# The first norm of the last token block: x turned on TensorE instead of loaded feature by feature

## The chip, the core and the metric

The kernel runs on one core of a Trainium2 chip. The metric is the device time of one execution in microseconds (us). Before the change it is 2847.49 us, the median of three runs (2845.23 to 2849.25).

## What is computed

One layer of an encoder: 2048 tokens, 1024 features, all float32. The part around the change is the first norm and what takes it up:

```python
def rms_norm(x, g):
    xf = x.astype(jnp.float32)
    y = xf * lax.rsqrt(jnp.mean(xf * xf, axis=-1, keepdims=True) + EPS)
    return (y * g.astype(jnp.float32)).astype(x.dtype)

def modulate(h, shift, scale):
    return h * (1 + scale) + shift
...
        h = modulate(rms_norm(x, norm_g[i, 0]), sh_m, sc_m)
        if m == 0:
            y = stick_breaking_mixer(h, sb_w_qkv[r], sb_w_o[r])
...
    qkv = (h @ w_qkv).reshape(b, s, 3, N_HEADS, HEAD_DIM)
```

`stick_breaking_mixer` is an attention of 16 heads whose weights come from sigmoids of the scores and a running product along the keys, in blocks of 128 queries. It is followed by an output projection, a gate and a gated feed-forward layer.

## The kernel before, in words

Every product is done in two or three passes on float32 data split into a high part (rounded) and a low part (the rest): a high and a low half are kept side by side in one tile, and `mm3` (lines 176 to 178) runs high x high, high x low, low x high. So each operand costs a rounding copy (high) and a subtraction (low) on some engine.

The tokens are cut into four blocks of 512 (b = 0 to 3), the features into eight groups of 128 (k = 0 to 7), the heads into eight pairs. `project` makes keys (t = 1), queries (t = 0) and values (t = 2) of one pair and one block: eight slices of three matmuls each, `pj`. The projections of pair 0 for blocks 0 to 3 come first. Beside them the norm of the next block is made, and with block 1 the attention of pair 0 begins: from then on slices of projections and stages of attention alternate in a fixed order that is written out by hand (`ORDER_IN_SLOT`). All four compute engines issue in exactly the order in which the program records their instructions; only the DMA queue SP is ordered by the framework.

The stages of attention, for each 128 queries and 512 keys: `score` (TensorE, `z`, line 604), `sigmoids` (ScalarE, two passes: `a` line 621, `z` in place line 623), `break_sticks` (VectorE scan into `w`, lines 633 and 638; then GpSimd multiplies `a` by it, line 645), `turn` (TensorE transposes, `t`, line 655), `split_high` (ScalarE copy, `aT`, line 665), `split_low` (VectorE subtraction, `aT`, line 671), `weigh_values` (TensorE, `o`, line 683). The values are turned as well (`vt`, line 552) and split (`v`, lines 556 and 557).

PSUM has eight banks of 128x512: three for the scores (`z`), two for the turned weights (`t`) and three (`acc`) shared by the projection (`pj`), the attention output (`o`), the turned values (`vt`) and, where there are any, the turned x (`xT`).

The norm has two ways. Blocks 0 and 2 go by tokens: x is loaded with tokens on the partitions, squared and summed on ScalarE (line 167), scaled by its reciprocal root on VectorE (line 349, 128x1024 each) and turned on TensorE, one feature group at a time (`x_turn`, line 372). For block 2, ScalarE then applies scale and shift (`hf`, line 394), and VectorE makes the high part (line 395) and the low part (line 396). Blocks 1 and 3, those in `BY_FEATURES`, go by features: x is also loaded with features on the partitions (`cols_load`, line 324, four DMAs `xc`), the reciprocal roots are spread over 128 columns (line 351), turned once (`xr`, line 363) and copied to SBUF (line 365). Each feature group is then multiplied by that row, on VectorE for even k (line 383) and on GpSimd for odd k (line 387). The modulated high part is ScalarE's (line 400, or lines 405 and 406), the low part VectorE's (line 401) or, for odd k of block 3, GpSimd's (line 408).

`first_norm` does this for one group. For block 3 it is called for k = 0 to 2 during the values' slices of block 2 (`NORM_AT[3]`), and for k = 3 to 7 during the keys' slices of block 3, three slices ahead of the slice that needs the group.

Of the kernel before, what the change touches and what calls it, by code (L numbers as in the profile page):

```python
# [9 lines left out]
F32 = mybir.dt.float32  # L10
F32R = mybir.dt.float32r
AF = mybir.ActivationFunctionType
ALU = mybir.AluOpType
# [3 lines left out]
P = 128  # L17
D = 1024
S = 2048
KC = D // P  # L20
# [3 lines left out]
BT = 512  # L24
NB = S // BT
# [44 lines left out]

H2_STEP = 3

BY_FEATURES = (1, 3)

SQUARE_AT = [(0, 2), (0, 7), (2, 1), (2, 7)]

# [7 lines left out]
def f32(ap):  # L84
    return ap.bitcast(F32)
# [22 lines left out]
def hybrid_trunk_kernel(  # L108
# [16 lines left out]
    nc = tc.nc  # L125
# [57 lines left out]
    tps = ctx.enter_context(tc.tile_pool(name="tps", bufs=2, space=PSUM))  # L183
    accps = ctx.enter_context(tc.tile_pool(name="accps", bufs=3, space=PSUM))
# [136 lines left out]
    def cols_load(b):  # L321
        for m in range(KC // 2):
            cols = att.tile([P, 2, BT], F32, name=f"xc{b}_{m}", tag="kt", bufs=BUFS["kt"])
            nc.sync.dma_start(cols, xt[b // 2, :, 2 * m : 2 * m + 2])
            x_cols[b, 2 * m], x_cols[b, 2 * m + 1] = cols[:, 0], cols[:, 1]

    def x_square(b, i):
        if b > 0:
            tok = x_tiles[b, i]
            if b in BY_FEATURES:  # L330
                junk = tok
# [13 lines left out]
    def x_spread(b, i):  # L345

        if b not in BY_FEATURES:
            tok = x_norm[b, i] = x_tiles.pop((b, i))
# [6 lines left out]
    def x_share(b):  # L355

        if b not in BY_FEATURES:
            return
        pool, tag = (tps, "t") if b < 2 else (accps, "acc")
        pt = pool.tile([P, BT], F32, name=f"xr{b}", tag=tag)  # L360
        for i in range(4):
            tok = x_tiles.pop((b, i))
            nc.tensor.transpose(pt[:, i * P : (i + 1) * P], tok[:, :P], ident)
        x_row[b] = tok[:, BT:]
        nc.scalar.copy(x_row[b], pt)

    def x_turn(b, k):

        pool, tag = (tps, "t") if b == 0 else (accps, "acc")
        pt = pool.tile([P, BT], F32, name=f"xT{b}_{k}", tag=tag)  # L370
        for i in range(4):
            nc.tensor.transpose(
                pt[:, i * P : (i + 1) * P], x_norm[b, i][:, k * P : (k + 1) * P], ident
            )
        return pt

    def scale_cols(b, k):

        if b not in BY_FEATURES:
            return  # L380
# [8 lines left out]
    def modulate(hl, b, k):  # L389

        gain, add = g_eff[:, 0, k : k + 1], shift[:, 0, k : k + 1]
        if b not in BY_FEATURES:
            u = att.tile([P, BT], F32, name=f"hf{b}_{k}", tag="tmp", bufs=BUFS["tmp"])
            nc.scalar.activation(u, x_turn(b, k), AF.Identity, bias=add, scale=gain)
            nc.vector.tensor_copy(hl[:, 0], u)
            nc.vector.tensor_tensor(hl[:, 1], u, f32(hl[:, 0]), op=ALU.subtract)
            return
        u = x_cols.pop((b, k))
        if k % 2 == 0:
            nc.scalar.activation(hl[:, 0], u, AF.Identity, bias=add)  # L400
            nc.vector.scalar_tensor_tensor(
                hl[:, 1], u, add, f32(hl[:, 0]), op0=ALU.add, op1=ALU.subtract
            )
        else:
            nc.scalar.activation(u, u, AF.Identity, bias=add, scale=gain)
            nc.scalar.copy(hl[:, 0], u)
            eng = nc.gpsimd if b == NB - 1 else nc.vector
            eng.tensor_tensor(hl[:, 1], u, f32(hl[:, 0]), op=ALU.subtract)  # L408

    def h_load(p, b):  # L410
        h = []
# [8 lines left out]
    def first_norm(b, k):  # L420
        if b is None or k >= KC:
            return
        if k % 2 == 0:
            ht = att.tile([P, 2, 2, BT], F32R, name=f"ht0_{b}_{k // 2}", tag="ht", bufs=BUFS["ht"])
            norm_h.setdefault(b, []).extend([ht[:, 0], ht[:, 1]])
            norm_tile[b] = ht
        for ahead in range(0 if k == 0 else k + 2, min(k + 3, KC)):
            scale_cols(b, ahead)
        modulate(norm_h[b][k], b, k)
        if k % 2 == 1:  # L430
            nc.sync.dma_start(h_s[b][:, k - 1 : k + 1], f32(norm_tile[b]))
# [21 lines left out]
    def project(at):  # L453

        p, b = STEPS[at]
# [3 lines left out]
        nb = STEPS[at + 1][1] if at + 1 < len(STEPS) and STEPS[at + 1][0] == 0 else None  # L459
# [4 lines left out]
        def product(t):  # L464
            if begun:
                return first_acc[t]
            w = weights[p, t]
            if parked and t == 1:
                acc = zps.tile([P, BT], F32, name=f"pj{p}_{b}_{t}", tag="z")
            else:  # L470
                acc = accps.tile([P, BT], F32, name=f"pj{p}_{b}_{t}", tag="acc")
            ahead = b == NB - 1 and p + 1 < NPAIR
            for k in range(KC):
                if t == 1:
                    if p == 0:
                        first_norm(b, k + (4 if b == 1 else 3))
                    if k == 0 and nb == 3:
                        cols_load(3)
                    if k == 5 and waiting:
                        waiting.pop()()  # L480
                if parked and t == 1 and k % 2 == 0:
                    nc.sync.dma_start(*stores[k // 2])
                if parked and (t, k) == (1, 6):
                    split_early(1, 2, ["whl"])
                if nb in (1, 3) and t == 1 and k < 4:
                    x_square(nb, k)
                if nb and t == 1 and 2 <= k < 6:
                    x_spread(nb, k - 2)
                if nb == 2 and (t, k) == (0, 0):
                    x_load(3)  # L490
                if nb == 1 and (t, k) in SQUARE_AT:
                    x_square(2, SQUARE_AT.index((t, k)))
                if nb and (t, k) == (0, 1):
                    x_share(nb)
                if (t, k) in NORM_AT[nb]:
                    first_norm(nb, NORM_AT[nb].index((t, k)))
                if ahead and k == 0:
                    load_weights(p + 1, t)
                if ahead and k == 6:
# [34 lines left out]
        else:  # L534
# [311 lines left out]
    for q in range(4):  # L846
        m = 2 * q
# [632 lines left out]
    for n, (s, f) in enumerate(groups):  # L1480
# [3 lines left out]
        for at, product in enumerate(PRODUCTS):  # L1484
            acc = banks_of[{1: 0, 6: 0, 7: 0, 4: 0, 5: 1, 3: 1, 2: 2}[product]]
            for k in range(H4):
                hl, r = left[n - (n == FC), product], right[s, product, k]
# [3 lines left out]
                t = 4 * at + k  # L1491
# [220 lines left out]
```

## Time and profile before

| | us |
|---|---|
| median of three runs | 2847.49 |
| the profiled execution | 2847.32 |
| its span, first to last instruction | 2845.3 |
| TensorE busy in the span | 2797.2 |
| VectorE busy | 2025.0 |
| ScalarE busy | 1634.2 |
| GpSimd busy | 1288.2 |

PE is TensorE's matmuls, DVE is VectorE, ACT is ScalarE, POOL is GpSimd, SP is the queue that issues the DMAs. The granted TensorE clock is 0.999 of full speed on the mean. A timeline row gives start, duration (both us), engine, line of the kernel, operation, tiles written and read, their size and count; in brackets how long the engine was idle before it and what ended that. A wait row gives the waiting group, the one it waited for, the us in total, how many times, and the longest.

### The profile page before, as it was taken

How to read it: one execution, taken by the hardware profiler on the slowest of the kernel's cores; microseconds unless marked ns; L12 is line 12 of the kernel's file. 1: busy time of each engine (PE TensorE's matmuls, PEld its weight loads, DVE VectorE, ACT ScalarE, POOL GpSimd, SP SyncE). 2: the span in 40 equal slices, each digit the busy share in tenths (PEclk: the TensorE clock that was granted, in tenths of full speed). 3: DMA queues.
4: the chain of work that ended last, by engine and by line, in shares of the span. 5: the costliest groups of instructions: out<-in, count | busy, mean ns of one | idle time of the engine just before them, and what ended most of it. 6: DMA issues, size and time to landing. Idle time of an engine off the chain costs nothing.

```text
span 2845.3 us, 41773 instructions
## 1 busy us (share of the span) xinstructions
PE 2797.2 (98%) x13825; PEld 2335.3 (82%) x13825; DVE 2025.0 (71%) x2824; ACT 1634.2 (57%) x3275; POOL 1288.2 (45%) x2036
## 2 busy tenths in 40 slices
PE   8999999999999999999999999999999999999998
PEld 6788888888888888887888788888788888888887
DVE  6788898888888888888866766655776655133376
ACT  5787777788777877777645533333433333322233
POOL 1475666666575655657410122221222222544454
PEclk9999999999999999999999999999999999999999
DMA  9865547657565635646289644334453335545566
GB/s 359 291 219 167 189 151 231 210 170 235 182 211 193 202 123 179 201 127 236 80 304 313 207 137 152 123 94 161 134 175 110 111 105 166 191 139 154 181 212 200
DMA packets 240520, 521.04 MB, mean 183 GB/s; under 512 B 22448, under 2 KB 110512, under 8 KB 222640
## 3 DMA queue, kind: packets, MB, share of 16 engines
q1 hardware_dynamic: 240304, 518.38, 56.1%
q8 instruction: 109, 1.79, 0.3%
q14 instruction: 107, 0.88, 0.1%
HBM read 351.04 MB, written 118.49 MB: 165 GB/s over the span
## 4 chain that ended last, share of the span: by engine, by line
PE 85%; DVE 5%; issue 3%; ACT 2%; POOL 2%; DMA 2%; SPq 0%; DVEq 0%; POOLq 0%; ACTq 0%
PE s L176 9%; PE s L177 9%; PE s L178 9%; PE z L604 8%; PE o L683 8%; PE t L655 8%; PE pj L176 5%; PE pj L177 5%; PE pj L178 5%; PE o L178 4%; PE o L177 4%; PE o L176 4%; PE y L178 2%; PE y L176 2%; PE y L177 2%
## 5 line engine op out<-in xcount | busy, mean ns | idle before, releaser
L645 POOL TENSOR_TENSOR a<-a,w 128x512 f32<-128x512 f32 (+3 forms) x640 | 621.1, 970 | 225.3 <-DVE w L638 130.4
L638 DVE TENSOR_TENSOR_SCAN w<-z,c,begin 128x512 f32<-128x512 f32 x384 | 489.4, 1279 | 84.7 <-ACT z L623 62.1
L176 PE MATMUL s<-r,l 128*128 128x512 f32 x1232 | 481.8, 391 | 4.8 <-DVE p L1447 3.9
L178 PE MATMUL s<-r,l 128*128 128x512 f32 x1232 | 479.9, 389 | 0.0
L177 PE MATMUL s<-r,l 128*128 128x512 f32 x1232 | 479.8, 389 | 0.0
L621 ACT ACTIVATE a<-z 128x512 f32<-128x512 f32 (+3 forms) x640 | 347.1, 542 | 170.7 <-PE z L604 137.6
L683 PE MATMUL o<-aT,v 128*128 128x512 f32 (+3 forms) x1280 | 384.8, 382 | 0.1
L671 DVE TENSOR_TENSOR aT<-t,aT 128x512 fp32r<-128x512 f32 (+3 forms) x640 | 358.8, 595 | 23.7 <-ACT aT L665 23.1
L604 PE MATMUL z<-kt,qt 128*128 128x512 f32 (+3 forms) x1280 | 363.8, 366 | 0.1
L665 ACT CAST aT<-t 128x512 fp32r<-128x512 f32 (+3 forms) x640 | 314.0, 533 | 73.8 <-PE t L655 63.7
L623 ACT ACTIVATE z<-z 128x512 f32<-128x512 f32 (+3 forms) x640 | 345.5, 540 | 0.0
L1455 POOL TENSOR_TENSOR one<-p,p 128x512 f32<-128x512 f32 x44 | 71.5, 1624 | 576.7 <-issue 320.3
L176 PE MATMUL pj<-ht,w 128*128 128x512 f32 x768 | 309.5, 403 | 5.0 <-issue 1.4
L655 PE MATMUL t<-begin,a 128*128 128x128 f32 x2176 | 295.9, 274 | 14.1 <-DVE aT L671 12.9
L655 PEld LDWEIGHTS t<-begin,a 128*128 128x128 f32 x2176 | 255.5, 140 | 64.8 <-DVE aT L671 15.6
L177 PE MATMUL pj<-ht,w 128*128 128x512 f32 x768 | 303.7, 395 | 1.8 <-DVE ht L408 0.6
L178 PE MATMUL pj<-ht,w 128*128 128x512 f32 x768 | 303.3, 395 | 0.0
L176 PEld LDWEIGHTS s<-r,l 128*128 128x128 f32 x1232 | 231.3, 188 | 54.8 <-ACT l L1308 2.9
L178 PEld LDWEIGHTS s<-r,l 128*128 128x128 f32 x1232 | 231.3, 188 | 48.1
L177 PEld LDWEIGHTS s<-r,l 128*128 128x128 f32 x1232 | 231.4, 188 | 47.9 <-issue 0.5
L633 DVE TENSOR_TENSOR_SCAN w<-z,begin 128x128 f32<-128x128 f32 (+3 forms) x256 | 208.8, 818 | 77.0 <-ACT z L623 66.3
L604 PEld LDWEIGHTS z<-kt,qt 128*128 128x128 f32 x1280 | 230.6, 189 | 37.8 <-DVE w L633 0.5
(179 smaller groups left out, 4881.6 us busy)
## 6 DMA issues: line engine op xcount, KB each, us to landing
ht<-h_s SPq DMA_DIRECT2D x108, 1024.0 KB, 8.5
wi<-in_win SPq DMA_DIRECT2D x86, 512.0 KB, 4.0
qt<-qn SPq DMA_DIRECT2D x124, 256.0 KB, 4.9
ol_qt<-act_s SPq DMA_DIRECT2D x56, 512.0 KB, 3.9
act_s<-S SPq DMA_DIRECT2D x66, 256.0 KB, 3.9
br<-in_wout SPq DMA_DIRECT2D x66, 256.0 KB, 3.5
h_s<-ht SPq DMA_DIRECT2D x16, 1024.0 KB, 8.3
o_s<-os SPq DMA_DIRECT2D x128, 128.0 KB, 3.0
```

Source lines behind the costliest of these rows:

```text
L176: nc.tensor.matmul(acc, lhs[0], rhs[0], start=first, stop=False, **kw)
L177: nc.tensor.matmul(acc, lhs[0], rhs[1], start=False, stop=False, **kw)
L178: nc.tensor.matmul(acc, lhs[1], rhs[0], start=False, stop=last, **kw)
L604: nc.tensor.matmul(z[:, :n], q[:, e, part, r * P : (r + 1) * P], k[:, e, :n], start=part == 0, stop=part == 1,)
L621: nc.scalar.activation(a[:, :n], z[:, :n], AF.Sigmoid, scale=QK_SCALE)
L623: nc.scalar.activation(z[:, :n], z[:, :n], AF.Sigmoid, scale=-QK_SCALE)
L638: nc.vector.tensor_tensor_scan(rest[:, rev], left[:, rev], begin[:, :BT][:, rev], initial=carries[r], op0=ALU.mult, op1=ALU.bypass,)
L645: nc.gpsimd.tensor_tensor(a[:, :n], a[:, :n], rest[:, 1 : n + 1], op=ALU.mult)
L655: nc.tensor.transpose(pt[:, rb * P : (rb + 1) * P], weighed[i, rb][:, j * P : (j + 1) * P], ident)
L665: nc.scalar.copy(hl[:, 0, t0:], pt[:, t0:])
L671: nc.vector.tensor_tensor(hl[:, 1, t0:], pt[:, t0:], f32(hl[:, 0, t0:]), op=ALU.subtract)
L683: nc.tensor.matmul(acc[:, t0:], lhs, hl[:, part, t0:], start=sc == qb and j == 0 and part == 0, stop=sc == 0 and j == 3 and part == 1,)
```

## The change

Block 3 leaves `BY_FEATURES` and goes by tokens, like block 2, but with another split of the work: VectorE applies scale and shift straight from PSUM, ScalarE makes the high part, GpSimd the low part. The column loads of block 3, its spread roots and the row of roots are gone. The squares of block 3 are written to a tile of the `wraw` buffers instead of over x, since x is still needed.

```diff
-BY_FEATURES = (1, 3)
+BY_FEATURES = (1,)
...
-        pool, tag = (tps, "t") if b < 2 else (accps, "acc")
-        pt = pool.tile([P, BT], F32, name=f"xr{b}", tag=tag)
+        pt = tps.tile([P, BT], F32, name=f"xr{b}", tag="t")
...
         if b not in BY_FEATURES:
             u = att.tile([P, BT], F32, name=f"hf{b}_{k}", tag="tmp", bufs=BUFS["tmp"])
+            if b == NB - 1:
+                nc.vector.tensor_scalar(u, x_turn(b, k), gain, add, op0=ALU.mult, op1=ALU.add)
+                nc.scalar.copy(hl[:, 0], u)
+                nc.gpsimd.tensor_tensor(hl[:, 1], u, f32(hl[:, 0]), op=ALU.subtract)
+                return
             nc.scalar.activation(u, x_turn(b, k), AF.Identity, bias=add, scale=gain)
...
             nc.scalar.copy(hl[:, 0], u)
-            eng = nc.gpsimd if b == NB - 1 else nc.vector
-            eng.tensor_tensor(hl[:, 1], u, f32(hl[:, 0]), op=ALU.subtract)
+            nc.vector.tensor_tensor(hl[:, 1], u, f32(hl[:, 0]), op=ALU.subtract)
...
-                    if k == 0 and nb == 3:
-                        cols_load(3)
```

On TensorE 32 transposes of 128x128 come (eight groups of four) and four go; on VectorE eight passes come for eight; on ScalarE eight copies for twelve passes and the copy of the row; on GpSimd eight subtractions for four multiplications and four subtractions; on SP four loads of 512 KB go.

The order at three places, by the built programs. First VectorE during the keys' product of block 2, where the tokens of block 3 are scaled (`x3_2` and `x3_3` are the third and fourth 128 of them, `ht0_2` is block 2's normed x, `w1` and `t0` belong to attention units 1 and 0). Before:

```order
L396 TENSOR_TENSOR ht0_2_3_1016<-hf2_7_1036,ht0_2_3_1016 128x512
L351 TENSOR_SCALAR x3_2_795<-ones_68,n0_3_2_rstd_1000 128x128
L633 TENSOR_SCALAR w1_1_1050<-z1_1_1013,begin_62 128x256
L351 TENSOR_SCALAR x3_3_797<-ones_68,n0_3_3_rstd_1030 128x128
L633 TENSOR_SCALAR w1_2_1076<-z1_2_1057,begin_62 128x384
L671 TENSOR_TENSOR aT0_0_1083<-t0_0_1067,aT0_0_1083 128x512
L508 TENSOR_TENSOR kn0_2_1092<-pj0_2_1_929,kn0_2_1092 128x512
L671 TENSOR_TENSOR aT0_1_1104<-t0_1_1072,aT0_1_1104 128x384
```

and after (line numbers are one higher from there on):

```order
L400 TENSOR_TENSOR ht0_2_3_1011<-hf2_7_1032,ht0_2_3_1011 128x512
L349 TENSOR_SCALAR x3_2_795<-x3_2_795,n0_3_2_rstd_995 128x1024
L634 TENSOR_SCALAR w1_1_1046<-z1_1_1008,begin_62 128x256
L349 TENSOR_SCALAR x3_3_797<-x3_3_797,n0_3_3_rstd_1026 128x1024
L634 TENSOR_SCALAR w1_2_1072<-z1_2_1053,begin_62 128x384
L672 TENSOR_TENSOR aT0_0_1079<-t0_0_1063,aT0_0_1079 128x512
L509 TENSOR_TENSOR kn0_2_1088<-pj0_2_1_929,kn0_2_1088 128x512
L672 TENSOR_TENSOR aT0_1_1100<-t0_1_1068,aT0_1_1100 128x384
```

Nothing moves; the four scalings (two are shown) grow from 128x128 to 128x1024 in place.

Second, VectorE during the keys' product of block 3, where groups 5, 6 and 7 are made (`w5`, `t3`, `t4` are attention stages). Before:

```order
L638 TENSOR_SCALAR w5_0_1480<-z5_0_1460,c4_0_1369,begin_62 128x512
L671 TENSOR_TENSOR aT3_2_1487<-t3_2_1470,aT3_2_1487 128x512
L401 TENSOR_SCALAR ht0_3_3_1503<-xc3_3_946,shift_74,ht0_3_3_1503 128x512
L671 TENSOR_TENSOR aT3_3_1509<-t3_3_1475,aT3_3_1509 128x512
L638 TENSOR_SCALAR w5_1_1512<-z5_1_1492,c4_1_1392,begin_62 128x512
L638 TENSOR_SCALAR w5_2_1540<-z5_2_1521,c4_2_1416,begin_62 128x512
L671 TENSOR_TENSOR aT4_0_1547<-t4_0_1531,aT4_0_1547 128x512
```

and after:

```order
L639 TENSOR_SCALAR w5_0_1496<-z5_0_1470,c4_0_1374,begin_62 128x512
L672 TENSOR_TENSOR aT3_2_1503<-t3_2_1486,aT3_2_1503 128x512
L394 TENSOR_SCALAR hf3_5_1511<-xT3_5_1512,g_eff_73,shift_74 128x512
L394 TENSOR_SCALAR hf3_6_1525<-xT3_6_1526,g_eff_73,shift_74 128x512
L672 TENSOR_TENSOR aT3_3_1537<-t3_3_1491,aT3_3_1537 128x512
L639 TENSOR_SCALAR w5_1_1540<-z5_1_1508,c4_1_1397,begin_62 128x512
L394 TENSOR_SCALAR hf3_7_1552<-xT3_7_1553,g_eff_73,shift_74 128x512
L639 TENSOR_SCALAR w5_2_1574<-z5_2_1549,c4_2_1421,begin_62 128x512
L672 TENSOR_TENSOR aT4_0_1581<-t4_0_1565,aT4_0_1581 128x512
```

A pass over a turned group now stands ahead of each scan or subtraction there, where one low part stood. On ScalarE the copies `ht0_3` of these passes stand in the same way between the sigmoids and the high parts; before, its scalings of `xc` stood there.

Third, TensorE in the same slices. Before, two slices of the keys' product follow each other:

```order
L604 MATMUL z5_1_1492<-kt0_0_531,qt0_1_826 128x512 x2
L176 MATMUL pj0_3_1_1435<-ht0_3_1_1329,w0_1_279 128x512
L177 MATMUL pj0_3_1_1435<-ht0_3_1_1329,w0_1_279 128x512
L178 MATMUL pj0_3_1_1435<-ht0_3_1_1329,w0_1_279 128x512
L176 MATMUL pj0_3_1_1435<-ht0_3_1_1329,w0_1_279 128x512 [waits Activation_49]
L177 MATMUL pj0_3_1_1435<-ht0_3_1_1329,w0_1_279 128x512 [waits Pool_49]
```

and after (`xT3_5` and `xT3_6` are groups 5 and 6 of block 3, both in the same PSUM bank):

```order
L605 MATMUL z5_1_1508<-kt0_0_531,qt0_1_826 128x512 x2
L371 MATMUL xT3_5_1512<-begin_62,x3_0_791 128x128 [waits DVE_49]
L371 MATMUL xT3_5_1512<-begin_62,x3_1_793 128x128
L371 MATMUL xT3_5_1512<-begin_62,x3_2_795 128x128
L371 MATMUL xT3_5_1512<-begin_62,x3_3_797 128x128
L176 MATMUL pj0_3_1_1440<-ht0_3_1_1328,w0_1_279 128x512
L177 MATMUL pj0_3_1_1440<-ht0_3_1_1328,w0_1_279 128x512
L178 MATMUL pj0_3_1_1440<-ht0_3_1_1328,w0_1_279 128x512
L371 MATMUL xT3_6_1526<-begin_62,x3_0_791 128x128 [waits DVE_49]
L371 MATMUL xT3_6_1526<-begin_62,x3_1_793 128x128
L371 MATMUL xT3_6_1526<-begin_62,x3_2_795 128x128
L371 MATMUL xT3_6_1526<-begin_62,x3_3_797 128x128
```

Ahead of each slice stands a group of four transposes, and each group waits for VectorE: `xT3_3` to `xT3_7` are all given one bank of the `acc` pool, because the projection and the attention output hold the other two.

More of the change, by code (lines that the diff above doesn't have):

```diff
@@ L323, in cols_load @@
             cols = att.tile([P, 2, BT], F32, name=f"xc{b}_{m}", tag="kt", bufs=BUFS["kt"])
-            nc.sync.dma_start(cols, xt[b // 2, :, 2 * m : 2 * m + 2])
+            nc.sync.dma_start(cols, xt[:, 2 * m : 2 * m + 2])
             x_cols[b, 2 * m], x_cols[b, 2 * m + 1] = cols[:, 0], cols[:, 1]
@@ L1686 @@
         "x": get("x")[0],
-        "xt": get("x")[0].reshape(NB, BT, KC, P).transpose(0, 3, 2, 1)[1::2],
+        "xt": get("x")[0].reshape(NB, BT, KC, P).transpose(0, 3, 2, 1)[1],
         "c": get("c")[0].reshape(KC, P).T,
```

## The prediction

> **What bounds the kernel now.** I read the page first (busy time, then the chain that ended last), then the stretch that the change touches: by windows, by waits, by timeline.
>
> ```profile
> span 2845.3 us, 41773 instructions
> ...
> PE 2797.2 (98%) x13825; PEld 2335.3 (82%) x13825; DVE 2025.0 (71%) x2824; ACT 1634.2 (57%) x3275; POOL 1288.2 (45%) x2036
> ...
> PE 85%; DVE 5%; issue 3%; ACT 2%; POOL 2%; DMA 2%; SPq 0%; DVEq 0%; POOLq 0%; ACTq 0%
> ```
>
> TensorE is busy 98% and carries 85% of the chain, so a microsecond that it loses early is not won back later. It idles 48 us in all. Part of that lies where block 3 is normalised; the windows give the busy time of each engine in 8 us:
>
> ```profile
> core 0: us, PE busy (x) PEld busy (x) DVE busy (x) ACT busy (x) POOL busy (x), PEclk, DMA share, GB/s
> ...
> 100.00:108.00 8.00, 7.60 (x42) 5.82 (x41) 7.93 (x19) 7.09 (x18) 3.99 (x10) 1.00 0.96 292
> ...
> 116.00:124.00 8.00, 6.40 (x35) 5.17 (x35) 7.05 (x9) 6.33 (x14) 6.32 (x8) 1.00 0.84 254
> 124.00:132.00 8.00, 5.70 (x30) 4.47 (x29) 7.66 (x12) 5.97 (x15) 7.09 (x13) 0.86 0.44 164
> ...
> 140.00:148.00 8.00, 6.48 (x31) 4.38 (x30) 6.07 (x7) 6.73 (x14) 7.58 (x10) 1.00 0.54 196
> ...
> 156.00:164.00 8.00, 8.00 (x43) 6.78 (x42) 6.73 (x9) 6.98 (x14) 6.62 (x12) 1.00 0.82 288
> ```
>
> From 116 to 148 us TensorE has gaps in which VectorE, ScalarE and GpSimd are nearly full; from 156 it is full again. The wait view of 84 to 160 us (us in total, times, longest) puts nearly all of its gaps on one cause, and none on a DMA:
>
> ```profile
> PE t L655 <- DVE aT L671: 5.9, 4, 2.3
> ```
>
> The attention weights' transposes wait for the subtraction that frees their PSUM bank. So here the in-order queues of VectorE and ScalarE, which wait for each other, set the pace, and what the change puts **between** their instructions decides more than the work it adds to TensorE.
>
> **Transposes.** Eight groups of four come, the four of the reciprocal roots go. The timeline has both kinds, each with the matmul that starts after it:
>
> ```profile
> 98.17 0.66 PE L372 MATMUL xT<-begin,x 128*128 128x128 f32 x4 [0.35 <-ACT hf L394]
> 98.58 0.47 PE L176 MATMUL pj<-ht,w 128*128 128x512 f32 x1
> ...
> 105.07 0.62 PE L363 MATMUL xr<-begin,x 128*128 128x128 f32 x4
> 105.45 0.48 PE L176 MATMUL pj<-ht,w 128*128 128x512 f32 x1
> ```
>
> A group costs TensorE 98.58 - 98.17 = 0.41 us, the old one 0.38. The bare work is 8 x 0.41 - 0.38 = **+2.9 us**. It counts only where TensorE is the late one.
>
> **Scaling of the tokens (97 to 108 us).** Four VectorE instructions grow from 128x128 to 128x1024. By groups (us, mean ns):
>
> ```profile
> L349 DVE TENSOR_SCALAR x<-x,n_rstd 128x1024 f32<-128x1024 f32 x4 | 2.9, 741 | 0.0
> ...
> L351 DVE TENSOR_SCALAR x<-ones,n_rstd 128x128 f32<-128x128 f32 x8 | 2.2, 290 | 0.0
> ```
>
> and by timeline (start, duration) what stands behind them:
>
> ```profile
> 101.68 0.50 PE L177 MATMUL pj<-ht,w 128*128 128x512 f32 x1 [0.22 <-DVE ht L396]
> ...
> 106.92 0.49 PE L655 MATMUL t<-begin,a 128*128 128x128 f32 x3
> ...
> 104.82 0.67 DVE L671 TENSOR_TENSOR aT<-t,aT 128x512 fp32r<-128x512 f32 x1
> ...
> 106.00 0.55 DVE L671 TENSOR_TENSOR aT<-t,aT 128x384 fp32r<-128x384 f32 x1
> ```
>
> Each scaling grows by 0.741 - 0.290 = 0.45 us, four by 1.8, and VectorE is full there (7.93 of 8). The first stands ahead of the low part of block 2's seventh group, for which TensorE already waits (101.68): +0.46. All four stand ahead of the subtractions at 104.82 and 106.00, which free the banks for the three transposes at 106.92. The second subtraction ends at 106.55 + 1.8 = 108.35. TensorE, 0.46 late and 0.38 early for the lost group, reaches the third transpose at about 107.1 and waits 1.25. Sum: 0.46 - 0.38 + 1.25 = **+1.3 us**. Nothing hides it; behind it VectorE has gaps and catches up. Bounds: +0.1 if the scalings found a gap, +2.1 if one of them collides with GpSimd as below. ScalarE's squares keep their size. The four removed loads go from SP's queue, where the stores and the keys behind them are then earlier; no wait of TensorE there is on a DMA, so 0.
>
> **The new order from 116 to 149 us.** One 128x512 VectorE pass from PSUM to SBUF takes over scale and shift, then ScalarE copies, then GpSimd subtracts. The trace has no such multiply-add from PSUM. Nearest is a plain copy out of PSUM (first row), below it a copy within SBUF (second), above it ScalarE's own PSUM pass (third):
>
> ```profile
> L955 DVE COPY yh<-y 128x512 f32<-128x512 f32 x4 | 2.7, 673 | 0.5 <-ACT y_junk L935 0.5
> ...
> L395 DVE CAST ht<-hf 128x512 fp32r<-128x512 f32 x8 | 3.7, 464 | 2.7 <-ACT hf L394 2.7
> ...
> L394 ACT ACTIVATE hf<-xT,shift,g_eff x8: 770/779/790, 85.5 to 101.1; 128x512 f32<-128x512 f32 x8
> ...
> L406 ACT CAST ht<-xc x8: 619/621/625, 65.5 to 144.8; 128x512 fp32r<-128x512 f32 x8
> ```
>
> I take 0.67 (bounds 0.46 and 0.78) and 0.62 for the copy (fourth row). The other lengths, and how closely instructions follow each other, are in the timeline:
>
> ```profile
> 138.22 0.61 ACT L623 ACTIVATE z<-z 128x512 f32<-128x512 f32 x1
> 138.74 0.61 ACT L665 CAST aT<-t 128x512 fp32r<-128x512 f32 x1
> ...
> 139.77 1.27 DVE L638 TENSOR_TENSOR_SCAN w<-z,c,begin 128x512 f32<-128x512 f32 x1
> 140.97 0.66 DVE L671 TENSOR_TENSOR aT<-t,aT 128x512 fp32r<-128x512 f32 x1
> ```
>
> On one engine the next instruction starts some 0.1 us before the last one's end (139.77 + 1.27 against 140.97); to another engine I add 0.07. I walk in the times of before; the 1.3 us come on top. Three waits are new. ScalarE's copy waits for VectorE's pass, and the next scores' sigmoids stand behind that copy. VectorE's pass waits for the transposes, and the scans stand behind it. And **the transposes of one stretch share one PSUM bank** (the other two hold the projection and the attention output), so group k+1 waits for pass k, with the projection's and the scores' matmuls queued behind it.
>
> The rows of before against which I walk:
>
> ```profile
> 117.72 0.72 ACT L400 ACTIVATE ht<-xc,shift 128x512 fp32r<-128x512 f32 x1 [1.50 <-DVE xc L383]
> ...
> 121.51 0.96 PE L655 MATMUL t<-begin,a 128*128 128x128 f32 x7 [1.60 <-DVE aT L671]
> ...
> 128.21 0.33 PE L655 MATMUL t<-begin,a 128*128 128x128 f32 x1 [2.28 <-DVE aT L671]
> ...
> 129.49 1.09 POOL L645 TENSOR_TENSOR a<-a,w 128x512 f32<-128x512 f32 x1 [0.73 <-DVE w L638]
> ...
> 133.14 0.63 PE L552 MATMUL vt<-begin,vT 128*128 128x128 f32 x4
> ...
> 136.63 0.60 ACT L623 ACTIVATE z<-z 128x512 f32<-128x512 f32 x1
> ...
> 148.47 0.79 PE L655 MATMUL t<-begin,a 128*128 128x128 f32 x3
> ```
>
> *To 137 us.* Pass 0 ends at 117.6, so ScalarE's first copy starts at 117.7, as the row at 117.72 does now. VectorE is then quicker, and TensorE's wait before 121.5 shrinks from 1.6 to 0.4. That is given back: pass 1 stands behind the second scan and ends at 122.9; ScalarE idles for it from 120.6 to 123.0; its two sigmoids end at 124.6, the next scan at 126.0, a low part at 126.6, pass 2 at 127.1, its copy at 127.8, the next high part at 128.2 and its low part at 128.8. So the transpose of 128.21 starts at 128.9. The fourth scan ends at 130.5 and its GpSimd product at 131.7 where it was 129.49 + 1.09 = 130.6, so the values' transposes start at 134.15 for 133.14. The first three new groups lie inside these waits. The values' split (ScalarE from 134.9, VectorE to 136.2) now also frees the bank that the keys' projection takes; then pass 3 (to 136.8), its copy, a high part and two sigmoids: the sigmoid of the row at 136.63 ends at 138.97, not at 137.23. **+1.7 us.**
>
> *To 149 us.* From there one chain, by starts: scan 139.05, pass 4 140.24, copy 140.98, sigmoids 141.5 and 142.0, scan 142.67, low part 143.86, pass 5 144.44, transposes 6 145.18, pass 6 145.93, copy 146.67, high part 147.2, sigmoids 147.7 and 148.2, scan 148.84, pass 7 150.03, copy 150.78, sigmoids 151.3 and 151.8, scan 152.47, low parts 153.66 and 154.24. The last of the three transposes of the row at 148.47, now at about 148.95, then starts at 154.85: 15.9 us after the sigmoid's end, where it was 11.7. **+4.2 us**. TensorE's longest wait is that for pass 5, some 3 us. GpSimd's eight subtractions (1.27 us each by the row at 125.20 below) end inside these waits: 0, or +0.5 for the last one without that cover.
>
> **Sum.** 1.3 + 1.7 + 4.2 = 7.2 us; the 2.9 of transposes lie inside it. The profiled execution took 2847.3 us (its span and 2.0 around it; the median shown is 2847.5), so **2854.5**. Seven passes stand on the chain: by the bounds of one, -1.5 to +0.8.
>
> **Rivals.** *Collisions were the whole trouble (faster).*
>
> ```profile
> L383 DVE SCALAR_TENSOR_TENSOR xc<-xc,g_eff,x x8: 725/745/1673, 62.0 to 138.5; 128x512 f32<-128x512 f32 x8
> ...
> 125.34 1.67 DVE L383 SCALAR_TENSOR_TENSOR xc<-xc,g_eff,x 128x512 f32<-128x512 f32 x1
> ...
> 125.20 1.27 POOL L408 TENSOR_TENSOR ht<-xc,ht 128x512 fp32r<-128x512 f32 x1
> ```
>
> The removed VectorE operation takes 0.745 us in the median and 1.67 beside a GpSimd one. If that delay is what the transposes wait for, the 5.9 us go, and transposes and scalings stay: 2847.3 - 5.9 + 2.9 + 1.3 = 2845.6. Against it: my walk has no collision in it and still waits, because a pass between two scans holds ScalarE whatever its length. It wins if each pass and copy finds its input done when its turn comes. [...]
>
> *Only the work counts.* The waits stay as they are and nothing new is late: 2847.3 + 2.9 = 2850.2. Against it: one bank cannot take group 6 before pass 5 has read group 5.
>
> *The clock falls more.* Behind the waits of 120 to 128 us TensorE ran at half its clock (PEclk) for about 3 us:
>
> ```profile
> 130.00:131.00 1.00, 0.98 (x6) 0.87 (x6) 0.76 (x2) 0.87 (x2) 1.00 (x4) 0.50 0.86 234
> ```
>
> The walk counts that once, as before. If the 3 us wait for pass 5 brings it a second time, the 3 us of matmuls behind it take 6: 2857.5. Without it at all, 1.1 less than forecast. [...]
>
> **How the numbers follow.** The measurement can tell about 0.2% (5.7 us) from no change. Forecast 0.64, its own range 2851.5 to 2857.5, with 0.55 above 2853.2; only the work 0.17; collisions 0.09, of which 0.02 below 2841.8; clock 0.10. Slower 0.55 + 0.10 = 0.65; within 0.09 + 0.17 + 0.07 = 0.33; faster 0.02. The range 2848.5 to 2859 leaves out the collisions and the far ends of the others.
>
> **What would show it.** In the profile after: TensorE waiting for VectorE's pass ahead of the new transposes, longest near 3 us in the keys' product; ScalarE idle ahead of its copies; passes of about 0.67 us; the wait at 121.5 nearly gone; about 1.25 us of new wait near 107. It is wrong if a pass is far from 0.67, if the transposes find a free bank, or if TensorE is full from 116 to 149.

## The result, and the profile after

The changed kernel takes 2855.41 us (median of seven runs, 2853.85 to 2857.45) against 2847.49 before (seven runs, 2845.09 to 2849.25): a ratio of 1.0029, with a 95% interval of 1.0017 to 1.0040. It is slower by 7.9 us. The work of the engines has hardly changed: TensorE is busy 2800.3 us in a span of 2853.6 (3.1 us more than before, while the span is 8.3 longer), VectorE 2020.1, ScalarE 1631.2, GpSimd 1288.0.

Where the time went is found by following marks that both programs have. On TensorE's timeline of the changed kernel (start, duration, line, tiles, count, in brackets the idle time ahead and what ended it) the rows that answer to those shown of before are these, with two more of before below them:

```profile
98.69 0.66 PE L371 MATMUL xT<-begin,x 128*128 128x128 f32 x4 [0.35 <-ACT hf L398]
...
102.66 0.50 PE L177 MATMUL pj<-ht,w 128*128 128x512 f32 x1 [0.22 <-DVE ht L400]
...
108.95 0.33 PE L656 MATMUL t<-begin,a 128*128 128x128 f32 x1 [0.62 <-DVE aT L672]
109.04 0.71 PE L684 MATMUL o<-aT,v 128*128 128x512 f32 x2
...
123.12 0.96 PE L656 MATMUL t<-begin,a 128*128 128x128 f32 x7 [0.42 <-DVE aT L672]
...
131.14 0.30 PE L656 MATMUL t<-begin,a 128*128 128x128 f32 x1 [1.99 <-DVE aT L672]
...
147.24 0.66 PE L371 MATMUL xT<-begin,x 128*128 128x128 f32 x4 [2.97 <-DVE hf L394]
...
155.03 0.50 PE L177 MATMUL pj<-ht,w 128*128 128x512 f32 x1 [0.39 <-POOL ht L396]
156.60 0.79 PE L656 MATMUL t<-begin,a 128*128 128x128 f32 x3 [0.85 <-DVE aT L672]
157.15 0.71 PE L684 MATMUL o<-aT,v 128*128 128x512 f32 x2
```

```profile
107.16 0.71 PE L683 MATMUL o<-aT,v 128*128 128x512 f32 x2
...
149.02 0.71 PE L683 MATMUL o<-aT,v 128*128 128x512 f32 x2
```

Block 2's last turned group starts at 98.69 where it was 98.17: 0.52 us late. Of this 0.47 us is there by 74 us already (a projection matmul of block 1 starts at 74.10 for 73.63), ahead of the squares and scalings that the change alters. The low part of block 2 releases TensorE at 102.66 for 101.68, and the weighing `o` behind the third transpose starts at 109.04 for 107.16: 1.88 late, so 1.36 beyond the first half microsecond. The weighing at 157.15 was at 149.02: 8.13 late. The span ends 8.3 late. So nearly all of the loss, 8.13 - 0.52 = 7.61 us, lies between 98 and 157 us, in the stretch of the change, and it is never given back.

By windows of 8 us, with the same columns as before, the stretch with the longest wait is this:

```profile
140.00:148.00 8.00, 4.74 (x30) 3.54 (x29) 5.16 (x7) 3.60 (x7) 4.61 (x8) 1.00 0.33 133
```

From 140 to 148 us **every** engine is less busy than before: TensorE 4.74 for 6.48, VectorE 5.16 for 6.07, ScalarE 3.60 for 6.73, GpSimd 4.61 for 7.58. Nobody is full, and still all are late. That looks like engines that wait for each other. TensorE's waits of 84 to 165 us (us in total, times, longest), and then ScalarE's of 110 to 160, name them:

```profile
PE t L656 <- DVE aT L672: 5.0, 6, 2.0
PE xT L371 <- DVE hf L394: 3.3, 2, 3.0
PE pj L176 <- DVE v L558: 1.0, 1, 1.0
```

```profile
ACT ht L395 <- DVE hf L394: 14.9, 8, 2.4
```

All eight of ScalarE's new copies come too early and stand there, 14.9 us in all, with the sigmoids behind them. One turn of the loop can be read from two timelines, ScalarE's first, then VectorE's:

```profile
142.90 0.62 ACT L395 CAST ht<-hf 128x512 fp32r<-128x512 f32 x1 [2.05 <-DVE hf L394]
143.43 0.59 ACT L622 ACTIVATE a<-z 128x512 f32<-128x512 f32 x1
143.92 0.59 ACT L624 ACTIVATE z<-z 128x512 f32<-128x512 f32 x1
...
147.22 0.62 ACT L395 CAST ht<-hf 128x512 fp32r<-128x512 f32 x1 [2.20 <-DVE hf L394]
```

```profile
142.08 0.79 DVE L394 TENSOR_SCALAR hf<-xT,g_eff,shift 128x512 f32<-128x512 f32 x1
144.60 1.28 DVE L639 TENSOR_TENSOR_SCAN w<-z,c,begin 128x512 f32<-128x512 f32 x1 [1.73 <-issue]
145.80 0.67 DVE L672 TENSOR_TENSOR aT<-t,aT 128x512 fp32r<-128x512 f32 x1
146.38 0.81 DVE L394 TENSOR_SCALAR hf<-xT,g_eff,shift 128x512 f32<-128x512 f32 x1
```

The copy of 142.90 waits for the pass of 142.08; the two sigmoids behind it end at 143.92 + 0.59 = 144.51; only then can VectorE scan, at 144.60 (the view calls the 1.73 us "issue", but the scan reads the `z` that ScalarE has just written). Behind the scan and a low part comes the next pass, at 146.38, and for that the next copy has waited 2.20 us. One turn takes 147.22 - 142.90 = 4.3 us, and TensorE's 2.97 us at 147.24 is a part of it.

### The profile page after: what moved, and what is told of

The parts are those of the page before. It is cut to its first block, busy times and chain, and to the rows that moved or that the text cites. A ratio compares the mean times of both kernels' runs of the same rounds, so it can differ in the third digit from the quotient of the medians.

```text
span 2853.6 us, 41832 instructions
## 1 busy us (share of the span) xinstructions
PE 2800.3 (98%) x13853; PEld 2336.7 (82%) x13853; DVE 2020.1 (71%) x2824; ACT 1631.2 (57%) x3270; POOL 1288.0 (45%) x2036
## 4 chain that ended last, share of the span: by engine, by line
PE 85%; DVE 4%; issue 2%; ACT 1%; DMA 1%; POOL 1%; SPq 0%; DVEq 0%; POOLq 0%; ACTq 0%
PE s L176 9%; PE s L178 9%; PE s L177 9%; PE z L605 8%; PE o L684 8%; PE t L656 8%; PE pj L176 5%; PE pj L178 5%; PE pj L177 5%; PE o L178 4%; PE o L176 4%; PE o L177 4%; PE y L178 1%; PE y L176 1%; PE y L177 1%
## 6 DMA issues: line engine op xcount, KB each, us to landing
o_s<-os SPq DMA_DIRECT2D x128, 128.0 KB, 2.5
```

## The experiments

Runs differ by up to 3.3 us before the change's stretch is reached (block 2's last turned group starts at 96.55 us in one run and at 99.82 in another). So beside the medians I read each profile from that start: how much later the weighing behind the three transposes near 107 us comes (mark 1), and that behind the three near 148 us (mark 2). One profile is one execution: those of four kernels lie 2.7 to 4.4 us under the median of their runs (copy a slice later, scores' banks, unread transposes, plain pass). The last column says for how long, between the start and mark 2, TensorE ran at half its clock (PEclk 0.50). The same work took twice as long there: in the changed kernel eight transposes start 1.56 us ahead of the next matmul at 133.64, in the half clock, and 0.79 us at 140.68, at full clock. By my estimate from these the half clock can have cost up to half its length (1.7 us of 3.4), and differences between marks are only as sure as that.

| kernel | median, us | before beside it | ratio, 95% | start | mark 1 | mark 2 | half clock, us |
|---|---|---|---|---|---|---|---|
| before | 2847.49 | | | 98.17 | 8.99 | 50.85 | 3.4 |
| changed | 2855.41 | 2847.49 | 1.0017 to 1.0040 | 98.69 | 10.35 | 58.46 | 3.4 |
| copy a slice later | 2846.92 | 2846.92 | 0.9990 to 1.0007 | 97.01 | 10.36 | 48.99 | 0 |
| scores' banks | 2855.98 | 2846.92 | 1.0019 to 1.0041 | 96.55 | 10.36 | 58.53 | 6.8 |
| pass on ScalarE | 2846.24 | 2846.92 | 0.9987 to 1.0005 | 96.88 | 10.35 | 49.80 | 0 |
| unread transposes in before | 2849.52 | 2846.92 | 0.9996 to 1.0014 | 96.82 | 8.94 | 49.60 | 0 |
| copy and scalings later | 2843.66 | 2845.67 | 0.9979 to 0.9997 | 96.61 | 8.35 | 47.00 | 0 |
| the same, pass on ScalarE | 2844.88 | 2845.67 | 0.9982 to 1.0000 | 96.64 | 8.34 | 49.10 | 0.5 |
| plain pass | 2855.43 | 2845.67 | 1.0020 to 1.0041 | 96.63 | 10.36 | 56.98 | 6.8 |
| split of block 2 | 2849.24 | 2845.67 | 1.0002 to 1.0020 | 99.82 | 10.36 | 52.16 | 0 |
| last low part on VectorE | 2842.47 | 2846.29 | 0.9979 to 0.9997 | 96.67 | 8.30 | 45.52 | 0 |
| only scalings later | 2851.85 | 2846.29 | 1.0012 to 1.0030 | 96.60 | 8.34 | 56.32 | 3.4 |

**The theory** is that of the prediction: ScalarE and VectorE stop each other, because a copy that waits for a pass stands ahead of sigmoids, and a pass stands behind scans that wait for these sigmoids. **The rivals**: the turned groups' work on TensorE, the one PSUM bank that they share, the length of the pass.

### The copy a slice later

```diff
-                nc.scalar.copy(hl[:, 0], u)
-                nc.gpsimd.tensor_tensor(hl[:, 1], u, f32(hl[:, 0]), op=ALU.subtract)
+                copies.append((hl, u, b, k))
...
+                    late_copy()
```

> The changed kernel, but for block 3 ScalarE's copy, GpSimd's subtraction and the store of a group are recorded one projection slice later than VectorE's pass; the same instructions otherwise. Theory (the queues of ScalarE and VectorE stop each other: the sigmoids stand behind a copy that waits for a pass, the pass behind a scan that waits for the sigmoids): ScalarE's 14.9 us of waits for passes mostly go, the sigmoid of 140.26 starts by 138.5 and the last of the three transposes of 157.07 by 153; 3 to 5 us under the changed kernel, 2850.5 to 2852.5. Rival 1 (the TensorE work of the turned groups is the cost): the work is the same, 2855.4. Rival 2 (the shared bank is the cost): the transposes still wait about 3 us for a pass at 147, 2855 within 0.8.

2846.92 us, the same as the kernel before it was timed beside. ScalarE's waits, then TensorE's, then TensorE's timeline, of this kernel:

```profile
ACT ht L417 <- DVE hf L394: 1.8, 2, 1.5
```

```profile
PE pj L177 <- POOL ht L418: 1.1, 1, 1.1
...
PE t L670 <- DVE aT L686: 0.8, 2, 0.6
```

```profile
97.01 0.66 PE L371 MATMUL xT<-begin,x 128*128 128x128 f32 x4 [0.35 <-ACT hf L397]
...
146.00 0.71 PE L698 MATMUL o<-aT,v 128*128 128x512 f32 x2
```

The same instructions, with the copies, low parts and stores one slice later on their queues, and mark 2 is 58.46 - 48.99 = 9.5 us earlier. ScalarE's waits for passes fall from 14.9 to 1.8 us, and the transposes of the turned groups no longer wait 2.97. That settles the cause: the loss is in the order of the queues. That it is the copies which count, among the three kinds that moved, is read from the turn above, where the scan starts right behind the sigmoids that stood behind a copy. I had expected 3 to 5 us; it was twice that. The waits that the kernel before has (5.9 us of `t` for `aT`, 0.8 here) go as well, and TensorE's clock stays at 1.00 throughout, which is worth up to 1.7 us of it.

### The scores' banks for the turned groups

```diff
+        if b == NB - 1 and k >= 3:
+            pool, tag = zps, "z"
```

> The changed kernel, but the turned groups 3 to 7 of block 3 take banks of the scores' pool (three banks) instead of the pool that they share with projection and attention output. Theory (the order in the queues is the cost, the one bank only adds to it): the 2.97 us wait of the transposes for a pass goes from its place, but sigmoids, copies, passes and scans still follow each other in the same order; the last of the three transposes starts 0.5 to 1.5 us before 157.07, 2854 to 2855. Rival (one bank is the whole cost of 140 to 157): the 2.97 us and what stands behind it go, 4 us less, about 2851.4. A third way: the scores now wait for a bank, and the time is over 2855.4.

2855.98 us, no gain. ScalarE's waits, then TensorE's timeline:

```profile
ACT ht L397 <- DVE hf L396: 13.9, 7, 2.4
```

```profile
144.71 0.66 PE L373 MATMUL xT<-begin,x 128*128 128x128 f32 x4 [1.67 <-DVE w L641]
...
150.23 0.73 PE L607 MATMUL z<-kt,qt 128*128 128x512 f32 x2 [0.62 <-DVE w L641]
...
155.08 0.71 PE L686 MATMUL o<-aT,v 128*128 128x512 f32 x2
```

The wait for the pass has gone from its place and a wait for a scan has come: the three banks of the scores are freed by the same stopped queue. ScalarE's copies still wait 13.9 us for passes (14.9 in the changed kernel), so the stop is there without the one bank. The transposes of group 6 start 48.16 us behind the start mark instead of 147.24 - 98.69 = 48.55, and at mark 2 that 0.4 us is gone too. In this run the clock was also at half for longer (128.0 to 134.9 us, 6.8 us against 3.4 in the changed kernel), which may hide up to 1.7 us. My theory had expected 0.5 to 1.5 us from the bank; the median shows none of it, but this run can't exclude it. It does exclude the rival's 4 us.

### The pass on ScalarE

```diff
-                nc.vector.tensor_scalar(u, x_turn(b, k), gain, add, op0=ALU.mult, op1=ALU.add)
+                nc.scalar.activation(u, x_turn(b, k), AF.Identity, bias=add, scale=gain)
```

> The changed kernel, but scale and shift of block 3 are ScalarE's, from PSUM, as in block 2; copy and low part stay where the change put them. Theory (the stop between ScalarE and VectorE is the cost): the copy stands right behind its own pass on the same queue and VectorE's scans behind nothing; 8 x 0.78 = 6.2 us of work come to ScalarE, but its 14.9 us of waits go; the last of the three transposes starts by 154, 2851 to 2853. Rival 1 (work and bank are the cost, whoever does the pass): ScalarE's pass is as long as VectorE's, 2855.4 within 0.8. Rival 2 (ScalarE is the full engine): 6.2 us more work on it make it later than the change, over 2856.

2846.24 us, better than the theory's 2851 to 2853; TensorE's timeline, and the window in which the changed kernel was emptiest:

```profile
146.68 0.71 PE L684 MATMUL o<-aT,v 128*128 128x512 f32 x2
```

```profile
140.00:148.00 8.00, 7.81 (x43) 6.16 (x43) 5.60 (x7) 7.97 (x18) 5.97 (x9) 1.00 0.81 295
```

Mark 2 is 8.7 us earlier (up to 1.7 of it for the clock), although ScalarE has eight passes more and is full (7.97 of 8, for 3.60): it is busy with work and not with waiting. So the loop can be cut on either side, at ScalarE's copy or at VectorE's pass. A full engine was cheaper here than two half-empty ones that stop each other.

### The transposes alone, in the kernel before

```diff
+            if b == NB - 1:
+                unread.append(tok)
...
+        if b == NB - 1:
+            pt = accps.tile([P, BT], F32, name=f"un{b}_{k}", tag="acc")
+            for i in range(4):
+                nc.tensor.transpose(pt[:, i * P : (i + 1) * P], unread[i][:, :P], ident)
```

> The kernel before, with eight groups of four 128x128 transposes of block 3's tokens added ahead of each group of its norm, into the bank pool that the change uses; nobody reads them, and all else stays. Theory (the transposes lie inside waits that are there already): from 110 us on most of 3.3 us is hidden, 0.3 to 1.5 us more, 2847.8 to 2849. Rival (only the work counts: TensorE is 98% busy and pays each group): 8 x 0.41 = 3.3 us more, 2850.8.

2849.52 us beside 2846.92, an interval of -1.1 to +4.0 us, which tells neither from the other. The profile (2846.36 us, one of the faster executions) tells more of this stretch. TensorE's waits and its timeline:

```profile
PE t L663 <- DVE aT L679: 2.6, 2, 1.9
```

```profile
146.42 0.71 PE L691 MATMUL o<-aT,v 128*128 128x512 f32 x2
```

The waits for `aT` are 2.6 us instead of 5.9: most of the 3.3 us of added transposes lie in them. Mark 2 is 1.25 us earlier than before, not later, in a run whose clock never fell in this stretch (1.00 from 84 to 164 us; before it was at half for 3.4 us, worth up to 1.7). So the added work costs at most 1.7 - 1.25, about 0.5 us, here, and the work of the turned groups is not what the change costs; by the interval, too, it is no more than 4.0 of the 7.9 us.

### Copy and scalings later

On top of the copy a slice later:

```diff
-                if nb and t == 1 and 2 <= k < 6:
+                if nb and t == (0 if nb == 3 else 1) and 2 <= k < 6:
                     x_spread(nb, k - 2)
```

> The kernel with copy, low part and store a slice later, and besides the four scalings of block 3's tokens recorded in the slices of block 2's queries instead of its keys; the same instructions. Measured from the start of block 2's last turned group, the first weighing behind the three transposes near 107 us starts 8.99 us later in the kernel before, 10.35 in the changed one, 10.36 with the copy later; the one behind the three transposes near 148 us 50.85, 58.46 and 48.99. Theory (the scalings cost 1.36 because they stand ahead of two subtractions that free banks): 9.0 and 47.6; 1.4 us under the kernel with only the copy later, 2.5 to 3.5 under the kernel before, 2843.5 to 2844.5. Rival (the 1.8 us of scalings are VectorE work that has to be paid wherever it stands): 9.0, but 49.0 behind, no gain in the time.

2843.66 us. TensorE's timeline:

```profile
96.61 0.66 PE L371 MATMUL xT<-begin,x 128*128 128x128 f32 x4 [0.35 <-ACT hf L397]
...
104.96 0.71 PE L698 MATMUL o<-aT,v 128*128 128x512 f32 x2
...
143.61 0.70 PE L698 MATMUL o<-aT,v 128*128 128x512 f32 x2
```

Mark 1 is 8.35, 2.0 us less than with the scalings in their old place, and mark 2 is 2.0 less as well: nothing of the scalings comes back, and the rival falls. The gain is larger than my 1.36, and mark 1 is 8.99 - 8.35 = 0.64 earlier than before, for two reasons. The turned reciprocal roots of before, 0.38 us of TensorE ahead of mark 1, are gone. And the first of the four short spreads of before (0.29 us each) stood ahead of the low part that TensorE waits for: from the start to that matmul it is 101.68 - 98.17 = 3.51 us before and 3.31 here.

### The same with the pass on ScalarE

> As the kernel with copy and scalings later, but scale and shift of block 3 on ScalarE instead of VectorE. Theory (with the copy a slice later nobody stops for the pass any more, so it matters little which engine makes it): within 1 us of that kernel, first weighing behind the three transposes at 47 to 48.5 us. Rival (ScalarE, 7.0 to 8.0 of 8 us busy where it made the pass itself from 132 to 148, is full): 1 to 3 us above it, 49 to 50.5.

The three edits above together: 2844.88 us, 1.2 above the kernel just shown, with runs that overlap. TensorE's waits:

```profile
PE pj L177 <- POOL ht L418: 1.8, 2, 1.6
```

Mark 2 is 49.10, 2.1 us later, as the rival has it (the clock had fallen 0.5 us ahead of it). The longest wait for a low part is 1.6 us instead of 1.1, and waits of 0.4 us for a scan and 0.3 for `aT` have come. As far as one profile and overlapping runs can tell, ScalarE is the tighter place, once nobody stops for the pass any more.

### A plain copy as the pass

```diff
-                nc.vector.tensor_scalar(u, x_turn(b, k), gain, add, op0=ALU.mult, op1=ALU.add)
+                nc.vector.tensor_copy(u, x_turn(b, k))
```

> The changed kernel, but VectorE's pass of block 3 is a plain copy from PSUM: scale and shift of that block are left out. Theory (the pass costs 0.79 instead of the 0.67 of a copy because of its two operations with a column each, and seven of them lie on the chain): passes of 0.67, the weighing of 58.46 us at 57.6, 0.8 us under the changed kernel. Rival 1 (order alone decides, not the length of the pass): 58.4. Rival 2 (what makes the pass long is that it reads PSUM beside other engines): passes stay at 0.79, 58.4.

2855.43 us, no difference in the median; mark 2 is 1.5 us earlier in the profile, the fastest of the seven executions (2851.06 us), although the clock fell twice there. Groups on `hf`, of this kernel and then of the changed one (ns shortest/median/longest):

```profile
L394 DVE COPY hf<-xT x8: 665/674/692, 116.8 to 148.7; 128x512 f32<-128x512 f32 x8
```

```profile
L394 DVE TENSOR_SCALAR hf<-xT,g_eff,shift x8: 784/792/814, 118.9 to 152.2; 128x512 f32<-128x512 f32 x8
```

The two operations of the pass cost 0.12 us over a copy from PSUM, and reading PSUM at this place does not: the plain pass takes 674 ns in the median, the copy out of PSUM of the kernel before (L955, elsewhere in the program) 668 (rival 2 falls). What this does to the whole is not settled: the profile speaks for the shorter pass, the median for no difference.

### The split of block 2

```diff
-            if b == NB - 1:
-                nc.vector.tensor_scalar(u, x_turn(b, k), gain, add, op0=ALU.mult, op1=ALU.add)
-                nc.scalar.copy(hl[:, 0], u)
-                nc.gpsimd.tensor_tensor(hl[:, 1], u, f32(hl[:, 0]), op=ALU.subtract)
-                return
```

> The changed kernel, but block 3 is split as block 2 is: ScalarE scale and shift from PSUM, VectorE both copy and low part, GpSimd nothing. Theory (ScalarE and VectorE stop each other): ScalarE has no instruction left that waits for VectorE's pass, but VectorE's scans now stand behind copies that wait for ScalarE, with 0.9 us of VectorE work for each group instead of 0.8; the weighing of 58.46 us at 52 to 55, 2849 to 2852. Rival 1 (any turned group costs as much, whoever splits it): 58.5, 2855.4. Rival 2 (only a ScalarE that waits for a pass costs): 49 to 50, as with scale and shift on ScalarE, 2846 to 2847.

2849.24 us; on TensorE's timeline:

```profile
151.98 0.71 PE L679 MATMUL o<-aT,v 128*128 128x512 f32 x2
```

Mark 2 is 151.98 - 99.82 = 52.16, within what the theory gave. Five sixths of the loss go (6.3 of 7.6 us), although each group is still turned on TensorE; 2.4 us remain over the kernel with pass and copy on ScalarE. VectorE is busy 28.5 of 30 us from 118 to 148, and a part of that is a collision come back. Its low parts (ns shortest/median/longest):

```profile
L395 DVE TENSOR_TENSOR ht<-hf,ht x8: 691/1078/1605, 120.5 to 148.1; 128x512 fp32r<-128x512 f32 x8
```

Four of the eight, those beside a GpSimd product (at 120.53, 125.39, 139.99 and 148.13), took 1.46 to 1.60 us; the others took 0.69. What of the 2.4 us is this, and what is waiting, the run does not tell.

### Two finer steps

> The changed kernel with nothing but the scalings of block 3's tokens moved from the slices of block 2's keys to those of its queries. Theory (the scalings' place is a loss of its own, ahead of the stop between ScalarE and VectorE): the weighing near 107 us 8.35 us behind block 2's last turned group, as in the kernel with copy and scalings later, instead of 10.35, and all that comes behind it earlier by the same: 56.5 us instead of 58.46, about 2853.4. Rival (the queues from 116 us on take their pace from elsewhere, the early loss is swallowed): 8.35 and 58.5, 2855.4.

2851.85 us, with the edit of the scalings and no other:

```profile
96.60 0.66 PE L371 MATMUL xT<-begin,x 128*128 128x128 f32 x4 [0.35 <-ACT hf L398]
...
104.94 0.71 PE L684 MATMUL o<-aT,v 128*128 128x512 f32 x2
...
143.01 0.66 PE L371 MATMUL xT<-begin,x 128*128 128x128 f32 x4 [2.97 <-DVE hf L394]
...
152.92 0.71 PE L684 MATMUL o<-aT,v 128*128 128x512 f32 x2
```

Mark 1 is 2.0 us less and mark 2 is 2.1 less; the 2.97 us wait stands as it was. So the two losses are separate and add up: what is late ahead of the loop stays late behind it.

The other step, on top of the copy and scalings later:

```diff
-            nc.gpsimd.tensor_tensor(hl[:, 1], u, f32(hl[:, 0]), op=ALU.subtract)
+            eng = nc.vector if k == KC - 1 else nc.gpsimd
+            eng.tensor_tensor(hl[:, 1], u, f32(hl[:, 0]), op=ALU.subtract)
```

> As the kernel with copy and scalings later, but the low part of group 7, the last one, is VectorE's instead of GpSimd's. There a projection matmul waits 1.14 us for that low part, which stands behind a product on GpSimd. Theory: VectorE makes it before 141 us, the wait goes, the scan behind it is 0.6 us later in a gap of VectorE; the weighing behind the three transposes at 46 to 46.5 us instead of 47.0, 0.5 to 1 us less in the time, 2842.7 to 2843.2. Rival: the later scan frees the attention's next stage later, 47.0 or more.

2842.47 us beside 2846.29 of the kernel before, and by TensorE's timeline:

```profile
96.67 0.66 PE L371 MATMUL xT<-begin,x 128*128 128x128 f32 x4 [0.35 <-ACT hf L397]
...
142.19 0.71 PE L699 MATMUL o<-aT,v 128*128 128x512 f32 x2
```

Mark 2 is 45.52, another 1.5 us less and more than I had expected; TensorE's wait of 1.1 us for that low part is gone. This version, the whole change with its scalings, copies, low parts and stores recorded later and one low part on another engine, beats both kernels: by 3.8 us in the medians the one before (0.9979 to 0.9997, which is 0.9 to 6 us), by about 13 us the changed one up to mark 2.

## Why the prediction was right

*The first half microsecond.* It is not in the sum and hardly of the change: nearly all of it is there by 74 us, and starts differ by more than that from run to run.

*The scalings.* Forecast +1.3, measured +1.36 (+0.46 at the low part of block 2, as forecast). The forecast wait of 1.25 us comes in two pieces, with 0.20 and 0.62 us of idle in brackets; the brackets count from the end of the matmul ahead, and matmuls that do not wait start before that end (the projection's last 0.40 us there and start 0.23 apart), so the starts are the better measure. The scalings' place was the reason, as the last experiments show: moved, the loss goes and does not come back.

*To 137 us.* Forecast +1.7. The sigmoid of the row at 136.63 starts at 140.26, 3.63 late for 1.88 at the mark before it: +1.75.

```profile
140.26 0.60 ACT L624 ACTIVATE z<-z 128x512 f32<-128x512 f32 x1
```

The wait ahead of the seven transposes shrank from 1.60 to 0.42, as forecast (0.4), and was given back, with 0.96 and 1.99 us ahead of the next transposes in place of 2.28. The 0.96 us of the keys' projection for the low part of `v` came too.

*To 149 us.* Forecast +4.2, measured 8.13 - 3.63 = +4.5. The walk had pass 4 at 140.24 and pass 5 at 144.44; with the 1.88 us on top that is 142.12 and 146.32, and they started at 142.08 and 146.38. The wait for pass 5 was 2.97 us where some 3 were said.

*The term that was mis-sized* is the pass: 0.67 taken, 0.78 the upper bound, 0.79 measured. The nearest row was a copy, and the two operations with a column each came on top of it. The walk was 0.3 us short from the sigmoid on, and it fell behind by about 0.1 us at each of passes 4 to 7 (pass 5 started 0.06 late against it, the next two at 147.94 and 152.17, 0.13 and 0.26 late), which fits 0.12 us a pass. From engine to engine the walk added 0.07 us; the turn above shows 0.03 from pass to copy (142.87 to 142.90) and 0.09 from sigmoid to scan (144.51 to 144.60). That seven lie on the chain was a bound, and no run settles it: with the plain pass the median did not move. GpSimd's last low part held TensorE for 0.39 us at 155.03, but the transposes behind waited 0.85 us for VectorE anyway, so it cost nothing.

*A reason that was too broad* is the bank. The prediction let group k+1 wait for pass k because of one bank, and that was so; but with three banks the time did not fall, and ScalarE waited nearly as long. The bank passed the delay on to TensorE, it did not make it. The prediction also called three engines nearly full from 116 to 148 us that were busy 6.0 to 7.7 of 8 us in its own windows; what counted was that they waited.

*The rivals.* Only the work (2850.2): put into the kernel before, at least 2.8 of 3.3 us of transposes disappeared in waits, by the one profile. The collisions did go, and the time rose all the same. GpSimd's products near the change, before (110 to 150 us) and then after (116 to 157; ns shortest/median/longest):

```profile
L645 POOL TENSOR_TENSOR a<-a,w x14: 411/1093/1624, 109.8 to 148.0; 128x512 f32<-128x512 f32 x9, 128x256 f32<-128x256 f32 x2, 128x384 f32<-128x384 f32 x2, 128x128 f32<-128x128 f32 x1
```

```profile
L646 POOL TENSOR_TENSOR a<-a,w x12: 415/1092/1098, 119.1 to 156.1; 128x512 f32<-128x512 f32 x9, 128x128 f32<-128x128 f32 x1, 128x256 f32<-128x256 f32 x1, 128x384 f32<-128x384 f32 x1
```

The longest fell from 1624 to 1098 ns. The passes were not stretched: seven of the eight ran 0.5 us or more beside a GpSimd product or subtraction, the one at 137.93 ran beside none, and all eight took 784 to 814 ns. The clock fell once, for 3.4 us as before, and not behind the wait of 2.97 us, so that rival did not come. Its price was too high in the prediction, though: a half clock of 3.4 us, with the work twice as long in it, holds 1.7 us of full-speed work, so by my estimate a second one of that length adds at most 1.7 us and not 3.

What the prediction did not see is that the loss is not the price of the new split as such, but of this split recorded at these places: the same change with copies and scalings later costs nothing or gains, and with the pass on ScalarE the places can stay.

## What to carry to other kernels

When a chain of small steps is spread over engines that run their instructions in the recorded order (here VectorE's from the scan at 144.60 to the low part at 155.88 ran as the built program lists them), write out for each new instruction what stands behind it in its queue while it waits, and whether one of those is what the awaited engine needs next; if so, record it later or keep two steps of the chain on one engine. A window in which every engine is less busy than before and the end is later was the sign of such a loop here. The price of an added wait is read from the turn of that loop (4.3 us here), not from the length of the added work.

## What the hardware showed that I had not expected

In these runs the half clock did not follow the length of one wait alone. In the changed kernel TensorE idled 2.97 us ahead of 147.24 and its clock stayed at 1.00; it had fallen earlier, near 132 us. With the plain pass it idled 2.84 us ahead of 143.95, and then it fell. The changed kernel's row first, then those of the plain pass:

```profile
131.00:132.00 1.00, 0.86 (x5) 0.80 (x6) 0.51 (x1) 1.00 (x4) 0.50 (x2) 0.98 0.81 328
```

```profile
143.95 0.66 PE L371 MATMUL xT<-begin,x 128*128 128x128 f32 x4 [2.84 <-DVE hf L394]
...
144.00:145.00 1.00, 1.00 (x7) 0.92 (x8) 0.36 (x1) 0.54 (x1) 0.38 (x1) 1.00 0.00 0
145.00:146.00 1.00, 1.00 (x5) 0.76 (x4) 0.33 (x1) 0.63 (x2) 0.91 (x1) 0.60 0.00 0
146.00:147.00 1.00, 1.00 (x5) 0.70 (x4) 0.50 (x1) 1.00 (x3) 0.94 (x1) 0.50 0.31 131
```

The shorter wait was followed by a half clock, 1.3 us after it ended. The places of the falls say more. A window's PEclk tells when in it the clock changed: with full clock ahead and half behind, 0.60 is a fall at 145.2 us, 0.98 one at 131.96. By such windows the half clock lasted 3.4 us each time in this stretch, 129.8 to 133.2 us before, 132.0 to 135.4 in the changed kernel, 128.1 to 131.6 and 145.2 to 148.6 with the plain pass, and 6.8 us, twice as long, with the scores' banks. The two falls of the plain pass start 17.1 us apart, which is five times 3.41. From these lengths I estimate that the clock changed here at the ends of equal steps of 3.41 us, which ran on between the falls; one distance in one execution is all that speaks for the second half of it.

On steps so estimated the two waits differ. Counted back from 145.2, the step ahead of the fall begins at 141.8, and 2.2 us of the wait (141.1 to 143.95) lie in it. Counted on from 131.96 in the changed kernel, a step ends at 145.6 and parts the wait of 2.97 us (144.3 to 147.2) into 1.3 and 1.6 us. In the step ahead of the fall of before, 126.4 to 129.8, TensorE idled 1.8 us, though its longest wait was 2.28. Whether idle time in a step brings the fall, and how much of it, was not tested.
